# Places for raw weights apart, and six down matmuls between a slab's last two products

## The chip, the cores and the metric

The kernel runs on one core of a Trainium2 chip. It is timed in microseconds of device time, as the median of several runs. A profiled execution has its own time, and its trace gives the start and end of each instruction: TensorE (PE) multiplies, VectorE (DVE) and ScalarE (ACT) do elementwise work, GpSimd (POOL) does little here, and SyncE (SP) issues the loads from memory. Each engine takes its instructions strictly in one order.

## The reference

Two layers, each of an FFN, a mixer and a second FFN, every one followed by a residual sum and a layer norm. The sequence has 512 rows, the model width is 1024, the FFN width 2816.

```python
for l in range(DEPTH):                       # DEPTH = 2
    h = 0.5 * _swiglu(x, w_gate[l, 0], w_up[l, 0], w_down[l, 0])
    x = _layernorm(ALPHA * x + h, ...)
    h = _mixer(x, w_in[l], ..., w_out[l])    # convolution, LRU and windowed attention side by side
    x = _layernorm(ALPHA * x + h, ...)
    h = 0.5 * _swiglu(x, w_gate[l, 1], w_up[l, 1], w_down[l, 1])
    x = _layernorm(ALPHA * x + h, ...)

def _swiglu(x, wg, wu, wd):
    return (silu(x @ wg) * (x @ wu)) @ wd
```

All is float32. Gate and up are 1024 x 2816, down is 2816 x 1024, w_in 1024 x 1792 (14 column tiles of 128), w_out 1024 x 1024.

## The kernel before

**Split weights.** A float32 product is made of three products of a faster type. Each weight tile comes from memory as a raw tile of 128 x 1024 floats (512 KB). `split` makes its high part on ScalarE (`wh`, a cast, L131) and its low part on VectorE (`wl`, raw minus high, L132). Activations are held as high and low parts too (xT, sT, hH and hL). A product is then low weight by high activation, high weight by low activation, and high by high.

**Places.** `wpool` has 15 places of 128 x 1024 floats, which raw tiles, high and low parts, sums of raw tiles and partial results (`o`) share. `tpool` has 7 such places, for the raws of the gate and up weights and for scratch. PSUM has 8 banks of 128 x 512.

**Gate and up.** The FFN columns are handled as 11 pairs of blocks, in three slabs of 4, 4 and 3 pairs. One pair n takes seven products, named p1, p2, q6, p5, p7, p4, q3 (`run`), each of 24 matmuls of 128 x 256 (L482 to L484) on sums of weight blocks and of activation blocks. Their weights are prepared some steps ahead (`prep`): a sum of raws on VectorE (L420) where there is one, and a split. p1, q6, p7 and p4 of a pair add up in the same bank: between them ScalarE copies what stands there (L511, L516, L518, L521). p4 and q3 of a pair come after p1 of the next pair, except at a slab's end, where p7, p4 and q3 of the last pair follow each other directly. `finish` then makes silu(gate) times up and splits it into hH and hL.

**Down.** After a slab's products, each of its blocks f of 128 rows of w_down is loaded and split (`load_rows`), and `rowmm` multiplies it with the four row blocks t of the activations, six matmuls of 128 x 512 for each (L106): two with hL and the high weight, then four with hH, by the low and the high weight in turn. The sums of a slab stand in eight banks, two for each t, and all of them were taken at once, behind q3. In an FFN's last slab the last four blocks of w_down (RESIDENT) are held in place, and `tail` calls `rows(t)` for one t after another, takes the norm of that row block (L290 to L306) and transposes it (L138) for the next stage, whose first weights are loaded in between (`nxt.load`).

**Order.** The program is written in one order, and a scheduler sets from it, before the kernel runs, the order on each engine. So an instruction can stand at another place than the text has it, and loads are issued on SyncE's queue as their places come free.

Of the kernel before, what the change touches and what calls it, by code (L numbers as in the profile page):

```python
# [11 lines left out]
F32 = mybir.dt.float32  # L12
# [6 lines left out]
P = 128  # L19
D = 1024  # L20
S = 512
NT = S // P
# [29 lines left out]
def tile_hymba(  # L52
# [26 lines left out]
    nc = tc.nc  # L79

    cpool = ctx.enter_context(tc.tile_pool(name="cpool", bufs=1))
    wpool = ctx.enter_context(tc.tile_pool(name="wpool", bufs=15))
    hpool = ctx.enter_context(tc.tile_pool(name="hpool", bufs=1))
    xpool = ctx.enter_context(tc.tile_pool(name="xpool", bufs=1))
    tpool = ctx.enter_context(tc.tile_pool(name="tpool", bufs=7))
# [6 lines left out]
    def nm(s):  # L92
        uid[0] += 1
        return f"{s}_{uid[0]}"

    def bank():
        return psum.tile([P, 512], F32, tag="ps", name=nm("ps"))
# [7 lines left out]
    def mm(o, a, b, start, stop):  # L105
        nc.tensor.matmul(o, a, b, start=start, stop=stop)  # L106
# [27 lines left out]
    def transposed(dst, q, j, src):  # L134

        pt = bank()
        for c in range(4):
            nc.tensor.transpose(pt[:, c * P:(c + 1) * P], src[:, c * P:(c + 1) * P], ident)  # L138
        sl = slice(j * P, j * P + P)
        split(dst[q][:, 0, :, sl], dst[q][:, 1, :, sl], pt.rearrange("p (c t) -> p c t", c=4))  # L140
# [179 lines left out]
    class Start:  # L320
# [6 lines left out]
        def load(self, n=1, pool=None):  # L327
            for _ in range(n):
                self.pairs.append(self.thunks.pop(0)(pool))
# [32 lines left out]
                    mm(pb[:, lo:hi], wh[:, k, :], mh, False, k == KC - 1)  # L362

    def fetch_raw(src):
        raw = wpool.tile([P, D], F32, tag="w", name=nm("raw"))
        nc.sync.dma_start(raw if len(src.shape) == 2 else raw.rearrange("p (k f) -> p k f", k=KC), src)
        return raw

    def load(src, pool=None, raw=None):
        raw = fetch_raw(src) if raw is None else raw  # L370
        if pool is None:
            hi = wpool.tile([P, D], F32R, tag="w", name=nm("wh"))
            lo = wpool.tile([P, D], F32R, tag="w", name=nm("wl"))
        else:
            hi = tpool.tile([P, D], F32R, tag="t", name=nm("wh"))
            lo = tpool.tile([P, D], F32R, tag="t", name=nm("wl"))
        split(hi, lo, raw)
        return hi, lo
# [5 lines left out]
        pair = load(cols(src, c), pool, raw)  # L384
        return [w.rearrange("p (k f) -> p k f", k=KC) for w in pair]

    def load_rows(src, c, pool=None):
        return load(src[c * P:(c + 1) * P, :], pool)

# [62 lines left out]
    def rowmm(ys, a, w, first, last):  # L454
        ah, al = a
        wh, wl = w
        for hf in range(2):
            sl = slice(hf * 512, (hf + 1) * 512)
            mm(ys[hf], al, wh[:, sl], first, False)
        for hf in range(2):  # L460
            sl = slice(hf * 512, (hf + 1) * 512)
            mm(ys[hf], ah, wl[:, sl], False, False)
            mm(ys[hf], ah, wh[:, sl], False, last)

    def ffn(l, i, idx, start, nxt, last, hooks={}):
        wd = w_down[l, i]
# [8 lines left out]
        def product(step, n, pb, first):  # L475
            src, q = A[step]
            wh, wl = pairs[n].ready.pop(step)
            for g in range(2):
                o = pb[:, g * HALF:(g + 1) * HALF]
                for k in range(4):  # L480
                    st = first and g == 0 and k == 0
                    nc.tensor.matmul(o, wl[:, g, k, :], src[q][:, 0, k, :], start=st, stop=False, skip_group_check=True)  # L482
                    nc.tensor.matmul(o, wh[:, g, k, :], src[q][:, 1, k, :], start=False, stop=False, skip_group_check=True)  # L483
                    nc.tensor.matmul(o, wh[:, g, k, :], src[q][:, 0, k, :], start=False, stop=k == 3, skip_group_check=True)  # L484

        for si, (n0, n1) in enumerate(SLABS):
            fin = si == len(SLABS) - 1
            f0, f1 = 2 * n0, 2 * n1
            hH = hpool.tile([P, HMAX, S], F32R, tag="hA", name=nm("hH"))
            hL = hpool.tile([P, HMAX, S], F32R, tag="hB", name=nm("hL"))  # L490

            def finish(n, which, tile_, s0):

                v = tile_.rearrange("p (b g s) -> p b g s", b=2, g=2)
                nc.scalar.activation(v[:, :, 0, :], v[:, :, 0, :], AF.Silu)
                nc.vector.tensor_tensor(v[:, :, 0, :], v[:, :, 0, :], v[:, :, 1, :], op=ALU.mult)  # L496
                f = 2 * (n - n0)
                sl = (slice(None), slice(f, f + 2), slice(s0, s0 + HALF))
                split(hH[sl], hL[sl], v[:, :, 0, :])

            def run(step, n):
                if step in ("p1", "p2", "p5"):
                    acc[step, n] = bank()
                pb = acc[{"p1": "p1", "q6": "p1", "p7": "p1", "p4": "p1", "p2": "p2", "p5": "p5", "q3": "p5"}[step], n]
                product(step, n, pb, step in ("p1", "p2", "p5"))
                if step == "p1":
                    outs[n] = [wpool.tile([P, D], F32, tag="w", name=nm("o")) for _ in range(2)]
                oa, ob = outs[n]
                lo, hi = slice(0, 512), slice(512, 1024)
                if step == "p1":  # L510
                    nc.scalar.copy(oa[:, lo], pb)  # L511
                elif step == "p2":
                    nc.vector.tensor_tensor(oa[:, lo], pb, oa[:, lo], op=ALU.add)
                    acc.pop(("p2", n))
                elif step == "q6":
                    nc.scalar.copy(oa[:, hi], pb)  # L516
                elif step == "p7":
                    nc.scalar.copy(ob[:, hi], pb)  # L518
                    nc.vector.tensor_tensor(ob[:, hi], acc["p5", n], ob[:, hi], op=ALU.subtract)
                elif step == "p4":  # L520
                    nc.scalar.copy(ob[:, lo], pb)  # L521
                    finish(n, 1, ob, HALF)
                elif step == "q3":
                    nc.vector.tensor_tensor(oa[:, hi], pb, oa[:, hi], op=ALU.subtract)
                    finish(n, 0, oa, 0)
                    acc.pop(("p5", n))
                    acc.pop(("p1", n))
                    outs.pop(n)

            m4 = []  # L530
            first = n0 + 1 if si == 0 else n0
            if si == 0:
# [18 lines left out]
            seq = []  # L551
# [5 lines left out]
            for m, (step, n) in enumerate(seq):  # L557
                while ready < min(len(seq), m + 1 + AHEAD):
                    st, k = seq[ready]
                    pairs[k].prep(st)  # L560
                    ready += 1
                    if st == "p5" and k + 1 < n1:
                        pairs[k + 1].raw(0, 0)
                        pairs[k + 1].raw(1, 0)
                run(step, n)
                if m4:
                    transposed(sT, 2, 2 - len(m4), m4.pop(0))
                if step == "q3" and n in hooks:
                    hooks[n]()
            if fin:  # L570
                extra.pop()
            ys = [[bank(), bank()] for _ in range(NT)]

            def hpair(f, t):
                return hH[:, f - f0, t * P:(t + 1) * P], hL[:, f - f0, t * P:(t + 1) * P]

            flow = f1 - RESIDENT if fin else f1
            for f in range(f0, flow):
                w = load_rows(wd, f)
                for t in range(NT):  # L580
                    rowmm(ys[t], hpair(f, t), w, f == f0, f == f1 - 1)
            if not fin:
                for t in range(NT):
                    for hf, sl in enumerate(HS):
# [2 lines left out]
                continue  # L587
            coef = ln_coef(idx)
            ws = [load_rows(wd, f) for f in range(flow, f1)]
            if nxt:  # L590
                nxt.load(3)
                nxt.load(1, None)

            def rows(t):
                for w, f in zip(ws, range(flow, f1)):
                    rowmm(ys[t], hpair(f, t), w, f == f0, f == f1 - 1)
                return ys[t]
# [3 lines left out]
    def mixer(l, idx, start, nxt):  # L601
# [305 lines left out]
        for u in range(U + 2):  # L907
            if u < U:
                scores(u)
            if u < 2:  # L910
                query(2 + u)
            if SLAB_FROM <= u < SLAB_FROM + 4:
                wo.append(load_rows(w_out[l], 4 + u - SLAB_FROM))
            if 0 <= u - 2 < U:
                weighted(u - 2)
            if u - 3 in closes:
                attn_out(closes[u - 3], wo)
            if 0 <= u - 1 < U:
                transpose_p(u - 1)
            point()  # L920
            if u < U:
                normalise(u)
# [7 lines left out]
    for l in range(DEPTH):  # L930
        phases += [(ffn, (l, 0, 3 * l), ffn_start(l, 0)), (mixer, (l, 3 * l + 1), mixer_start(l)),
                   (ffn, (l, 1, 3 * l + 2), ffn_start(l, 1))]
# [61 lines left out]
```

## Time and profile before

| | before |
|---|---|
| median of 3 runs | 1774.04 us (1771.74 to 1775.43) |
| profiled execution | 1780.14 us, span 1778.4 us |
| TensorE clock granted in it | 0.987 of full |
| TensorE busy | 1720.0 us, 97% |
| VectorE busy | 1278.1 us, 72% |
| ScalarE busy | 821.1 us, 46% |
| loaded from memory | 171.33 MB |

The span is from the first to the last instruction of the trace. A row of a timeline gives the start in the span and the duration, then the engine, the line, the operation and its tiles; in brackets stands how long the engine had been idle and what ended that. Lines of the profile are those of the kernel before. SPq is SyncE's queue as it issues loads.

### The profile page before, as it was taken

To read this page: it belongs to the slowest core of one execution; us is meant where nothing else is said; L and a number is where in the kernel's file an instruction comes from. 1 tells how busy PE (TensorE), PEld (TensorE's weight loads), DVE (VectorE), ACT (ScalarE), POOL (GpSimd) and SP (SyncE) were. 2 spreads that over 40 slices of the span, in tenths; PEclk is the share of its full clock that TensorE was granted. 3 is DMA by queue.
4 is the path that set the end of the run, shared out by engine and by line. 5 is a ranking of instruction groups with operands and counts; after the bars stand their busy time and mean duration, and the time that the engine had idled before them with its cause. 6 is when DMAs were issued, how large, how long until landed. Compare 5 with 4: busy or idle time off the path is not lost. (4 is left out here: it accounts for less than half of the span.)

```text
span 1778.4 us, 27912 instructions
## 1 busy us (share of the span) xinstructions
PE 1720.0 (97%) x11538; PEld 1546.7 (87%) x11538; DVE 1278.1 (72%) x1777; ACT 821.1 (46%) x1224; POOL 44.0 (2%) x76
## 2 busy tenths in 40 slices
PE   8999999999999999999999999999999999999997
PEld 8988989887679989979889899898875799898896
DVE  5856856779877856747688567576898877577485
ACT  4543533543854543434445335254457445255252
POOL 0200000010000000000000000000000000000000
PEclk9999999999899999999999999999998999999999
DMA  5341542321222432422324324223311244235122
GB/s 157 109 142 57 167 135 72 119 81 45 98 84 75 127 131 72 129 85 72 107 84 131 131 71 128 87 72 110 111 59 58 73 124 144 65 104 163 45 94 72
DMA packets 236840, 177.34 MB, mean 100 GB/s; under 512 B 9524, under 2 KB 219561, under 8 KB 236713
## 3 DMA queue, kind: packets, MB, share of 16 engines
q1 hardware_dynamic: 236712, 175.55, 32.1%
q8 instruction: 91, 1.49, 0.3%
q14 instruction: 37, 0.30, 0.0%
HBM read 171.33 MB, written 3.67 MB: 98 GB/s over the span
## 5 line engine op out<-in xcount | busy, mean ns | idle before, releaser
L132 DVE TENSOR_TENSOR wl<-raw,wh 128x1024 fp32r<-128x1024 f32 x268 | 324.9, 1221 | 156.3 <-ACT wh L131 114.2
L482 PE MATMUL ps<-xT,wl 128*128 128x256 f32 x1280 | 355.5, 278 | 10.8 <-ACT o L518 9.8
L483 PE MATMUL ps<-xT,wh 128*128 128x256 f32 x1280 | 353.3, 276 | 0.0
L484 PE MATMUL ps<-xT,wh 128*128 128x256 f32 x1280 | 353.2, 276 | 0.0
L131 ACT CAST wh<-raw 128x1024 fp32r<-128x1024 f32 x268 | 278.5, 1048 | 132.7 <-DMA raw<-in_ffn_w_down_dram 69.8
L132 DVE TENSOR_TENSOR wl<-t,wh 128x1024 fp32r<-128x1024 f32 x160 | 195.8, 1226 | 143.4 <-ACT wh L131 117.7
L106 PE MATMUL ps<-wl,hH 128*128 128x512 f32 x704 | 276.5, 393 | 4.2 <-DVE wl L132 4.2
L106 PE MATMUL ps<-wh,hH 128*128 128x512 f32 x704 | 275.5, 391 | 0.0
L482 PE MATMUL ps<-sT,wl 128*128 128x256 f32 x960 | 264.8, 276 | 4.9 <-ACT o L511 4.9
L484 PE MATMUL ps<-sT,wh 128*128 128x256 f32 x960 | 264.1, 275 | 0.0
L483 PE MATMUL ps<-sT,wh 128*128 128x256 f32 x960 | 264.1, 275 | 0.0
L131 ACT CAST wh<-t 128x1024 fp32r<-128x1024 f32 x160 | 167.6, 1055 | 201.2 <-DVE t L420 166.0
L482 PEld LDWEIGHTS ps<-xT,wl 128*128 128x128 f32 x1280 | 241.2, 188 | 15.2 <-ACT o L518 12.1
L483 PEld LDWEIGHTS ps<-xT,wh 128*128 128x128 f32 x1280 | 241.3, 188 | 0.3
L484 PEld LDWEIGHTS ps<-xT,wh 128*128 128x128 f32 x1280 | 241.1, 188 | 0.0
L106 PE MATMUL ps<-wh,hL 128*128 128x512 f32 x704 | 218.6, 392 | 4.7 <-ACT wh L131 4.7
L106 PE MATMUL ps<-xT,wh 128*128 128x256 f32 (+1 forms) x960 | 214.3, 318 | 2.2 <-DVE xT L132 2.2
L482 PEld LDWEIGHTS ps<-sT,wl 128*128 128x128 f32 x960 | 180.3, 188 | 6.6 <-ACT o L511 5.8
L484 PEld LDWEIGHTS ps<-sT,wh 128*128 128x128 f32 x960 | 180.2, 188 | 0.0
L483 PEld LDWEIGHTS ps<-sT,wh 128*128 128x128 f32 x960 | 180.2, 188 | 0.0
L106 PEld LDWEIGHTS ps<-xT,wh 128*128 128x128 f32 x960 | 159.2, 191 | 17.1 <-DVE xT L132 3.2
L106 PEld LDWEIGHTS ps<-wl,hH 128*128 128x128 f32 x704 | 132.9, 189 | 35.2 <-DVE wl L132 7.7
(165 smaller groups left out, 2345.7 us busy)
## 6 DMA issues: line engine op xcount, KB each, us to landing
raw<-in_ffn_w_down_dram SPq DMA_DIRECT2D x88, 512.0 KB
raw<-in_ffn_w_gate_dram SPq DMA_DIRECT2D x160, 256.0 KB
raw<-in_ffn_w_up_dram SPq DMA_DIRECT2D x160, 256.0 KB
raw<-in_w_in_dram SPq DMA_DIRECT2D x28, 512.0 KB
raw<-in_w_out_dram SPq DMA_DIRECT2D x16, 512.0 KB
raw<-in_ffn_w_gate_dram SPq DMA_DIRECT2D x8, 512.0 KB
raw<-in_ffn_w_up_dram SPq DMA_DIRECT2D x8, 512.0 KB
t<-in_ln_g_dram SPq DMA_DIRECT2D x6, 512.0 KB
```

The source lines that it names most:

```text
L106: nc.tensor.matmul(o, a, b, start=start, stop=stop)
L131: nc.scalar.copy(hi, src)
L132: nc.vector.tensor_tensor(lo, src, hi.bitcast(F32), op=ALU.subtract)
L482: nc.tensor.matmul(o, wl[:, g, k, :], src[q][:, 0, k, :], start=st, stop=False, skip_group_check=True)
L483: nc.tensor.matmul(o, wh[:, g, k, :], src[q][:, 1, k, :], start=False, stop=False, skip_group_check=True)
L484: nc.tensor.matmul(o, wh[:, g, k, :], src[q][:, 0, k, :], start=False, stop=k == 3, skip_group_check=True)
```

## The change

Four things. Raw tiles of w_down, w_in, w_out and of an FFN's first gate and up columns get two places of their own (`rpool`); `wpool` has 16 places, for all else. The first two raws of a slab's w_down are sent for at p1 of the slab's last pair. The split of block f0 is written ahead of p7 and the one of f0+1 behind q3. The six matmuls of (f0, t = 0) stand between p7 and p4, and the banks of a t are taken when it is first needed; behind q3 come the other t of f0 and f0+1 in a written order, then the blocks from f0+2 on as before.

```diff
-    wpool = ctx.enter_context(tc.tile_pool(name="wpool", bufs=15))
+    wpool = ctx.enter_context(tc.tile_pool(name="wpool", bufs=16))
+    rpool = ctx.enter_context(tc.tile_pool(name="rpool", bufs=2))
...
     def fetch_raw(src):
-        raw = wpool.tile([P, D], F32, tag="w", name=nm("raw"))
+        raw = rpool.tile([P, D], F32, tag="r", name=nm("raw"))
...
-    def load_rows(src, c, pool=None):
-        return load(src[c * P:(c + 1) * P, :], pool)
+    def load_rows(src, c, pool=None, raw=None):
+        return load(src[c * P:(c + 1) * P, :], pool, raw)
...
+            ys = {}
+            early = {}
+
+            def hpair(f, t):
+                return hH[:, f - f0, t * P:(t + 1) * P], hL[:, f - f0, t * P:(t + 1) * P]
+
+            def down(f, t):
+                if t not in ys:
+                    ys[t] = [bank(), bank()]
+                rowmm(ys[t], hpair(f, t), early[f], f == f0, f == f1 - 1)
...
+                if (step, n) == ("p1", n1 - 1):
+                    first_raw = {f: fetch_raw(wd[f * P:(f + 1) * P, :]) for f in (f0, f0 + 1)}
+                if m == len(seq) - 3:
+                    early[f0] = load_rows(wd, f0, None, first_raw.pop(f0))
+                if m == len(seq) - 2:
+                    down(f0, 0)
                 run(step, n)
...
-            ys = [[bank(), bank()] for _ in range(NT)]
-
-            def hpair(f, t):
-                return hH[:, f - f0, t * P:(t + 1) * P], hL[:, f - f0, t * P:(t + 1) * P]
-
             flow = f1 - RESIDENT if fin else f1
-            for f in range(f0, flow):
-                w = load_rows(wd, f)
+            early[f0 + 1] = load_rows(wd, f0 + 1, None, first_raw.pop(f0 + 1))
+            for f, t in ((f0, 1), (f0, 2), (f0 + 1, 0), (f0 + 1, 1), (f0 + 1, 2), (f0, 3), (f0 + 1, 3)):
+                down(f, t)
+            for f in range(f0 + 2, flow):
+                early[f] = load_rows(wd, f)
                 for t in range(NT):
-                    rowmm(ys[t], hpair(f, t), w, f == f0, f == f1 - 1)
+                    down(f, t)
```

What the scheduler makes of it is seen in the order of instructions on an engine: line, operation, what is written and what is read, with the shape. (Below line 80 the changed kernel's lines are one higher than before, so L131 and L132 are L132 and L133 there.)

The first slab's end on ScalarE, before. `wh_1042` is p4's weight, `wh_1071` q3's, `wh_1204` the first of w_down; L518 copies p7's result and L521 p4's.

```order
L131 CAST wh_1042<-t_121_1040 128x1024
L131 CAST wh_1071<-raw_920 128x1024
L518 COPY o_913<-ps_887 128x512
L521 COPY o_913<-ps_887 128x512
L131 CAST wh_1204<-raw_1202 128x1024
```

The same place with the change. `wh_1049` is p4's weight, `wh_1078` q3's, `wh_1107` block f0 of w_down, `wh_1213` f0+1, `wh_1267` f0+2; L519 and L522 are the copies.

```order
L132 CAST wh_1049<-t_123_1047 128x1024
L132 CAST wh_1078<-raw_927 128x1024
L132 CAST wh_1107<-raw_890 128x1024
L519 COPY o_920<-ps_894 128x512
L132 CAST wh_1213<-raw_892 128x1024
L132 CAST wh_1267<-raw_1265 128x1024
L522 COPY o_920<-ps_894 128x512
```

f0's cast has moved ahead of p7's copy and stands third, behind the casts for p4 and q3; those of f0+1 and f0+2 have moved ahead of p4's copy. VectorE's subtractions stand in the same order.

On TensorE at that place, before, p7's last matmul is followed directly by p4's first:

```order
L483 MATMUL ps_887<-sT_142,wh_1010 128x256
L484 MATMUL ps_887<-sT_142,wh_1010 128x256
L482 MATMUL ps_887<-xT,wl_1043 128x256
L483 MATMUL ps_887<-xT,wh_1042 128x256
L484 MATMUL ps_887<-xT,wh_1042 128x256
```

With the change (`ps_1137` and `ps_1138` are the banks of t = 0, `ps_1217` and `ps_1218` those of t = 1):

```order
L485 MATMUL ps_894<-sT_145,wh_1017 128x256
L107 MATMUL ps_1137<-wh_1107,hL_159 128x512
L107 MATMUL ps_1138<-wh_1107,hL_159 128x512
L107 MATMUL ps_1217<-wh_1107,hL_159 128x512
L107 MATMUL ps_1218<-wh_1107,hL_159 128x512
L107 MATMUL ps_1137<-wl_1108,hH_158 128x512
L107 MATMUL ps_1137<-wh_1107,hH_158 128x512
L107 MATMUL ps_1138<-wl_1108,hH_158 128x512
L107 MATMUL ps_1138<-wh_1107,hH_158 128x512
L483 MATMUL ps_894<-xT,wl_1050 128x256
```

Two matmuls of (f0, t = 1) have been put in as well: eight of 512 columns stand between p7 and p4.

The tail of the first FFN on VectorE, with the change. The L291 rows are the first row block's residual sums, L294 to L307 its norm, the L133 rows splits of the next stage's first weights:

```order
L133 TENSOR_TENSOR wl_3567<-raw_3564,wh_3566 128x1024
L291 SCALAR_TENSOR_TENSOR t_3606,zs_3607<-ps_3412,xs 128x512
L133 TENSOR_TENSOR wl_3573<-raw_3570,wh_3572 128x1024
L291 SCALAR_TENSOR_TENSOR t_3606,zs_3607<-ps_3413,xs 128x512
L133 TENSOR_TENSOR wl_3579<-raw_3576,wh_3578 128x1024
L294 TENSOR_SCALAR nmean_3610<-zs_3607 128x1
L305 SCALAR_TENSOR_TENSOR xs<-t_3606,nmean_3610,t_3530 128x512 x2
```

Before, the sums of two row blocks came together, with one split behind them; now the first block's sums stand alone, with splits between them.

The kernel's end on VectorE, before, has the sums of row blocks 0 and 1 together:

```order
L290 SCALAR_TENSOR_TENSOR t_16986,zs_16987<-ps_16866,xs 128x512
L290 SCALAR_TENSOR_TENSOR t_16986,zs_16987<-ps_16867,xs 128x512
L290 SCALAR_TENSOR_TENSOR t_17026,zs_17027<-ps_16868,xs 128x512
L293 TENSOR_SCALAR nmean_16990<-zs_16987 128x1
L290 SCALAR_TENSOR_TENSOR t_17026,zs_17027<-ps_16869,xs 128x512
L304 SCALAR_TENSOR_TENSOR xs<-t_16986,nmean_16990,t_16934 128x512 x2
```

With the change each row block's norm is through before the next one's sums:

```order
L291 SCALAR_TENSOR_TENSOR t_16989,zs_16990<-ps_16819,xs 128x512
L291 SCALAR_TENSOR_TENSOR t_16989,zs_16990<-ps_16820,xs 128x512
L294 TENSOR_SCALAR nmean_16993<-zs_16990 128x1
L305 SCALAR_TENSOR_TENSOR xs<-t_16989,nmean_16993,t_16937 128x512 x2
L307 SCALAR_TENSOR_TENSOR xs<-xs,rs_16995,t_16938 128x512 x2
L291 SCALAR_TENSOR_TENSOR t_17029,zs_17030<-ps_16889,xs 128x512
```

On TensorE the four resident blocks of w_down are taken for one row block after the other there, where those of row blocks 0 and 1 stood mixed.

## The prediction

> **What bounds the kernel now.** I read the page first, then the waits of TensorE, then the timelines of TensorE, ScalarE and VectorE around one slab end, then those around the last norms. The page:
>
> ```profile
> PE 1720.0 (97%) x11538; PEld 1546.7 (87%) x11538; DVE 1278.1 (72%) x1777; ACT 821.1 (46%) x1224; POOL 44.0 (2%) x76
> ```
>
> TensorE is busy nearly always, and the change removes no matmul. So it can only win from TensorE's stops, and from what lies behind its last matmul. The waits of TensorE (total, times, longest) list the stops:
>
> ```profile
> PE ps L482 <- ACT o L518: 9.8, 12, 1.7
> PE ps L138 <- DVE xs L306: 6.7, 5, 1.6
> PE ps L138 <- DMA xs<-in_x_dram: 6.0, 2, 4.5
> ...
> PE ps L106 <- ACT wh L131: 4.7, 7, 2.1
> PE ps L106 <- DVE wl L132: 4.2, 8, 0.5
> ...
> PE ps L106 <- DVE xT L132: 2.2, 4, 0.9
> ...
> PE ps L482 <- DVE wl L132: 1.0, 4, 0.3
> ```
>
> Rows 1, 4, 5 and 7 are the slab ends: twelve waits for p7's copy, then those of the first down matmuls for their weights. They make 19.7 us, plus about 0.17 at each stop, because a gap counts from the end of a 0.28 us matmul whose successor normally starts 0.11 us after its start. Start to start, the twelve slab ends lose 26.5 us by my count. The first of them, on TensorE, ScalarE, VectorE and SyncE's queue:
>
> ```profile
> 94.80 0.28 PE L483 MATMUL ps<-sT,wh 128*128 128x256 f32 x1
> 94.91 0.28 PE L484 MATMUL ps<-sT,wh 128*128 128x256 f32 x1
> 95.92 0.39 PE L482 MATMUL ps<-xT,wl 128*128 128x256 f32 x1 [0.73 <-ACT o L518]
> ...
> 98.78 0.28 PE L482 MATMUL ps<-sT,wl 128*128 128x256 f32 x1
> ...
> 101.39 0.28 PE L484 MATMUL ps<-sT,wh 128*128 128x256 f32 x1
> 102.54 0.73 PE L106 MATMUL ps<-wh,hL 128*128 128x512 f32 x2 [0.88 <-ACT wh L131]
> 103.80 0.50 PE L106 MATMUL ps<-wl,hH 128*128 128x512 f32 x1 [0.53 <-DVE wl L132]
> 104.14 0.39 PE L106 MATMUL ps<-wh,hH 128*128 128x512 f32 x1
> 104.37 0.39 PE L106 MATMUL ps<-wl,hH 128*128 128x512 f32 x1
> ```
>
> ```profile
> 92.90 1.06 ACT L131 CAST wh<-t 128x1024 fp32r<-128x1024 f32 x1 [2.43 <-DVE t L420]
> 93.86 1.05 ACT L131 CAST wh<-raw 128x1024 fp32r<-128x1024 f32 x1
> 95.28 0.59 ACT L518 COPY o<-ps 128x512 f32<-128x512 f32 x1 [0.38 <-PE ps L484]
> ...
> 101.44 1.04 ACT L131 CAST wh<-raw 128x1024 fp32r<-128x1024 f32 x1 [1.88 <-DMA raw<-in_ffn_w_down_dram]
> ```
>
> ```profile
> 93.99 1.23 DVE L132 TENSOR_TENSOR wl<-t,wh 128x1024 fp32r<-128x1024 f32 x1 [1.18 <-ACT wh L131]
> 95.13 1.22 DVE L132 TENSOR_TENSOR wl<-raw,wh 128x1024 fp32r<-128x1024 f32 x1
> 96.27 0.68 DVE L519 TENSOR_TENSOR o<-ps,o 128x512 f32<-128x512 f32 x1
> ```
>
> ```profile
> 96.83 1.42 SPq L366 DMA_DIRECT2D raw<-in_ffn_w_down_dram  x1
> ...
> 114.56 0.33 SPq L366 DMA_DIRECT2D raw<-in_ffn_w_down_dram  x1
> ```
>
> p7 is issued out at 95.02 (94.91 plus a step of 0.11). p4 adds into the same bank, so it waits for the copy: 0.90 lost. q3 ends at 101.50, but the first w_down raw was sent for only at 96.83, its cast starts 4.61 later, and TensorE loses 1.04 for the cast and 0.80 for the subtraction. Together 2.7 to 2.9 us.
>
> **The change part by part.** *Six down matmuls ahead of p4.* The copy is now covered: it runs while TensorE works on f0. But these matmuls need f0's own split, and the orders put that split last of three on both engines: behind p4's and q3's. In the rows above ScalarE is through q3's cast at 94.91, so f0's cast ends about 95.95: TensorE waits 0.93 from p7's end. It then does the four hL products (0.227 each, the step from 104.14 to 104.37): until 96.87. VectorE is through q3's subtraction at 96.35 (start 95.13, 1.22), so f0's ends about 97.52: 0.65 more. Four products, since the scheduler has put eight down matmuls there and not six: p4 starts at 98.43. From p7's end that is 3.41, of which 8 x 0.227 = 1.82 is work: lost 1.6. The wait has changed its name from the copy to f0's split. Behind q3 nothing is waited for any more, since f0 and f0+1 are split by then. So 2.87 becomes 1.61 here.
>
> The same reckoning elsewhere hangs on when q3's preparation ends against p7. Two other slab ends, the first of them the last slab of an FFN:
>
> ```profile
> 330.61 1.04 ACT L131 CAST wh<-raw 128x1024 fp32r<-128x1024 f32 x1
> 331.89 1.22 DVE L132 TENSOR_TENSOR wl<-raw,wh 128x1024 fp32r<-128x1024 f32 x1
> ...
> 748.09 1.22 DVE L132 TENSOR_TENSOR wl<-raw,wh 128x1024 fp32r<-128x1024 f32 x1
> ```
>
> With p7 ending at 330.31 and 747.57 the losses go from 1.91 to 3.09 and from 5.33 to 2.02. The eight slab ends that are not an FFN's last lose 21.8 before and 13.6 after. The four last ones have no wait behind q3 today (their raws came early), so only the copy, 0.92 in three of them: 4.7 before, 7.7 after. Sum: 26.5 to 21.3, **gain 5.2**. If the split came first on both engines, all of it would go; if it came a whole subtraction later, 12 x 1.14 more would be lost: bounds +26 and -9.
>
> *Two raw places.* A raw place is free again only after the subtraction, so loads go in pairs. One load takes 114.56 to
>
> ```profile
> 118.14 1.05 ACT L131 CAST wh<-raw 128x1024 fp32r<-128x1024 f32 x1 [3.63 <-DMA raw<-in_ffn_w_down_dram]
> ```
>
> that is 3.58 until its cast, up to 4.61 above, then 1.05 and 1.22: 5.9 to 6.9 for two, 2.9 to 3.4 each. A down step takes 24 x 0.227 = 5.45, so the stream keeps up: f0+2 is sent for at 97.5, ready near 104.5, and needed only at about 113. Cost 0 while that cover of 9 us lasts. The first raws of the next slab now stand in SyncE's queue ahead of that slab's later pair raws, and wait for the splits of the last w_down blocks, here at 121.1 and 122.3 with
>
> ```profile
> 119.84 2.48 DVE L132 TENSOR_TENSOR wl<-raw,wh 128x1024 fp32r<-128x1024 f32 x2 [4.07 <-PE ps L106]
> ...
> 128.73 0.38 SPq L412 DMA_DIRECT2D raw<-in_ffn_w_gate_dram  x1
> ```
>
> before the pair raw behind them was sent: 0, with 6 us of cover.
>
> *The inner tails (three).* rows(0) is now finished alone, 5.45 us ahead of rows(1), where both ended together. But two to four splits of the next stage's first loads stand before the first norm is through on VectorE, and they come by pairs. Before:
>
> ```profile
> 359.77 0.69 DVE L290 SCALAR_TENSOR_TENSOR t<-ps,xs 128x512 f32<-128x512 f32 x1 [11.50 <-PE ps L106]
> ```
>
> My reckoning with 3.58 per load gives 2.6 us of wait at the first transposes and 0.4 to 0.6 at the second, 3.2 a tail, where rows 2 and 6 of the waits and their restarts make 9.6 for three today. So 0. With loads of 4.6 it would be 2 more per tail; if the loads were in time, up to 3.2 less.
>
> *The kernel's end.* Before, rows(0) and rows(1) end together, and four norms run one after another on VectorE:
>
> ```profile
> 1766.26 0.39 PE L106 MATMUL ps<-wh,hH 128*128 128x512 f32 x1
> ```
>
> ```profile
> 1755.81 0.69 DVE L290 SCALAR_TENSOR_TENSOR t<-ps,xs 128x512 f32<-128x512 f32 x1 [12.37 <-PE ps L106]
> ...
> 1770.57 0.68 DVE L290 SCALAR_TENSOR_TENSOR t<-ps,xs 128x512 f32<-128x512 f32 x1
> ...
> 1773.81 1.41 DVE L306 SCALAR_TENSOR_TENSOR xs<-xs,rs,t 128x512 f32<-128x512 f32 x2 [0.84 <-POOL rs L297]
> ```
>
> The last matmul ends at 1766.65, the last norm at 1775.22, the span at 1778.4: 11.75 behind TensorE. From 1755.81 to 1775.22 is 4.85 a norm, and a row block of four weights takes 4 x 6 x 0.227 = 5.45: with the blocks finished one by one, three norms hide under matmuls. Left are one norm (1770.57 to 1775.22, 4.65, and 0.61 for its other half's sum) and the store, 3.2: 8.5. **Gain 3.3**; at least 0, at most 4.
>
> *Start and mixers.* Two of the first weights now go ahead of x's third block: 0 to one transfer, 1.4 (the 96.83 row): I take 0.5 lost. In the mixers
>
> ```profile
> raw<-in_w_in_dram SPq DMA_DIRECT2D x28, 512.0 KB
> raw<-in_w_out_dram SPq DMA_DIRECT2D x16, 512.0 KB
> ```
>
> go by pairs as well, where up to 15 places were open. A projection of one column tile takes 5.45, above 3.4, so 0, with one late load (4.6) per mixer as the bound on the one side and 2 per mixer gained on the other.
>
> **Sum:** -5.2 - 3.3 + 0.5 = -8.0: the profiled execution's 1780.1 becomes 1772. It lies 6.1 above the median of the runs, so the median 1774.0 becomes **1766**.
>
> **Rivals.** *A, the stops are cured.* If f0's split were in time, all 26.5 and the 3.3 would go: 1774 - 30 = 1744. For it speaks that 16 + 2 places replace 15; against it that q3's subtraction ends 1.2 us behind p7 in the rows above, with f0's behind that. It decides if ScalarE and VectorE run over 2 us earlier against TensorE than now. The Trainium skill (Perfetto Trace Analysis, Optimization Strategy) says that the same gap repeating on the engine that should be full can mean too few SBUF or PSUM places. By that, the added places would give this result; the trace disagrees at p4, where the releaser is a copy, and agrees only behind q3, where a raw came late.
>
> *B, two places are too few: slower.* Where a load's cast comes 4.6 and not 3.6 after its issue, each of three inner tails loses 2 more (6), and each mixer waits once for a load that was there before (9.2): -8 + 15.2 = +7, 1781. It decides from about 4.3. For it: the 4.61 measured with other transfers beside it, and engines that go strictly in order, so that one late raw stops every copy and norm behind it. Against it: 3.58 where the queue is idle, as in tails and mixers.
>
> *C, waits only change names.* The slab ends win 2 or less because the last slabs lose more than 3, and the end wins 1 or 2 because the norms now meet splits: 1771 to 1777. For it: the four last slabs already lose by my own count.
>
> **How the numbers follow.** About 0.2%, 3.5 us, is what can be told from no change. The forecast (1760 to 1770.5) has 0.50, A 0.10, C 0.18, B 0.22. So faster 0.60, same 0.18, slower 0.22. The range reaches from a third of the way to A to the near part of B, 1755 to 1780, which leaves out most of A and some of B.
>
> **What would show it.** In the waits: no row of p4 for L518's copy; in its place twelve waits of the hL products for ACT's wh (0.3 to 1.9 each) and twelve of the hH products for DVE's wl (about 0.7); none behind q3; about 21 us in all. At the end: the last VectorE norm about 5.3 behind the last matmul, where it is 8.6. In the tails: waits for xs of 2 to 3 us in total per tail. I am wrong if these waits are missing or twice as long, or if new waits for w_in or w_out show up in the mixers.

## The result

The changed kernel takes 1762.33 us (median of 4 runs, 1761.57 to 1765.92), the kernel before 1774.48 (median of 4, 1771.74 to 1775.43). The ratio is 0.9934, with a 95% interval from 0.9922 to 0.9947: 12.2 us faster, where 8.0 were forecast. The profiled execution of the changed kernel took 1762.13 us, with a span of 1760.4; that is its median, while the one of before lay 5.7 above its own. So the two traces differ by 18.0 us and the medians by 12.2.

The page of the changed kernel, where its engines are as busy as before:

```profile
PE 1709.4 (97%) x11538; PEld 1541.6 (88%) x11538; DVE 1279.2 (73%) x1777; ACT 819.8 (47%) x1224; POOL 39.5 (2%) x76
```

The waits of its TensorE, total, times and longest (its lines are one higher than before up to L525, and 12 to 18 higher behind that):

```profile
PE ps L107 <- ACT wh L132: 11.2, 12, 2.1
PE ps L139 <- DVE xs L307: 6.7, 3, 2.7
PE ps L139 <- DMA xs<-in_x_dram: 6.0, 2, 4.6
PE ps L107 <- DVE wl L133: 5.2, 12, 0.5
...
PE ps L107 <- ACT xT L132: 2.3, 1, 2.3
...
PE ps L483 <- DVE wl L133: 1.0, 4, 0.3
```

No product waits for p7's copy any more. In its place stand, at each of the twelve slab ends, one wait of the hL products for ScalarE's `wh` and one of the hH products for VectorE's `wl`. The first slab end, on TensorE, ScalarE and VectorE (start, duration, idle time before and what ended it):

```profile
95.84 0.28 PE L485 MATMUL ps<-sT,wh 128*128 128x256 f32 x1
96.88 1.20 PE L107 MATMUL ps<-wh,hL 128*128 128x512 f32 x4 [0.76 <-ACT wh L132]
98.52 0.50 PE L107 MATMUL ps<-wl,hH 128*128 128x512 f32 x1 [0.45 <-DVE wl L133]
...
99.56 0.28 PE L483 MATMUL ps<-xT,wl 128*128 128x256 f32 x1
```

```profile
94.84 1.98 ACT L132 CAST wh<-raw 128x1024 fp32r<-128x1024 f32 x2
96.73 0.58 ACT L519 COPY o<-ps 128x512 f32<-128x512 f32 x1
```

```profile
94.97 1.23 DVE L133 TENSOR_TENSOR wl<-t,wh 128x1024 fp32r<-128x1024 f32 x1 [1.12 <-ACT wh L132]
96.11 2.35 DVE L133 TENSOR_TENSOR wl<-raw,wh 128x1024 fp32r<-128x1024 f32 x2
```

The two casts from 94.84 are q3's and f0's, the two subtractions from 96.11 likewise. p7 is issued out at 95.95. p4 starts at 99.56, 3.61 later, of which 1.82 is work; 1.79 is lost.

The end of the kernel on TensorE and VectorE:

```profile
1751.97 0.39 PE L107 MATMUL ps<-wh,hH 128*128 128x512 f32 x1
```

```profile
1751.95 0.69 DVE L291 SCALAR_TENSOR_TENSOR t<-ps,xs 128x512 f32<-128x512 f32 x1 [0.17 <-PE ps L107]
...
1755.80 1.42 DVE L307 SCALAR_TENSOR_TENSOR xs<-xs,rs,t 128x512 f32<-128x512 f32 x2 [0.85 <-POOL rs L298]
```

One norm is left behind the last matmul.

**Where the time went.** The program has the same 11,538 matmuls before and after. So the time from the n-th to the m-th matmul can be compared directly. The second trace of before is that of run e0 below.

| Part of the program (matmul counts) | before | before, 2nd trace | changed | changed minus first |
|---|---|---|---|---|
| start and first products (0 to 620) | 80.10 | 80.04 | 80.92 | +0.8 |
| products with the bias table (930 to 1480) | 72.18 | 70.69 | 73.88 | +1.7 |
| eight slab ends that are not an FFN's last | | | | -8.8 |
| four last slabs with their tails | | | | +2.0 |
| first mixer's second half (2900 to 3340) | 100.03 | 97.53 | 95.35 | -4.7 |
| second mixer's (8560 to 9050) | 115.48 | 113.93 | 110.01 | -5.5 |
| behind the last matmul's start | 12.10 | 12.09 | 8.38 | -3.7 |

These sum to -18.2; the spans differ by -18.0. The mixers, costed at nothing, won 10.2 against the first trace of before and 6.1 against the second. At the slab ends the sum came out near the forecast, but not by stops alone. 4.8 of the 8.8 were won at one end, near 756 in the span, where TensorE waits 2.1 for f0's cast in the kernel before. Behind that wait the first trace shows a granted clock of 0.50 for 6.8 us (the window's busy times, then clock, DMA share and GB/s), in which the step between two down matmuls is 0.43 us and not 0.227:

```profile
757.00:763.80 6.80, 6.27 (x16) 4.88 (x16) 6.46 (x9) 5.53 (x7) 0.00 (x0) 0.50 0.64 233
```

The two other traces with the order of before show 3.4 us at 0.50 there, the changed kernel none. In the changed kernel the clock stood at 0.50 for 3.4 us from 335.3, behind a wait of 2.1 at the first FFN's last slab.

### The profile page after: what moved, and what is told of

Read it like the earlier page. It is cut to its first block, busy times and chain, and to the rows that moved or that the text cites. A ratio compares the mean times of both kernels' runs of the same rounds, so it can differ in the third digit from the quotient of the medians.

```text
span 1760.4 us, 27877 instructions
## 1 busy us (share of the span) xinstructions
PE 1709.4 (97%) x11538; PEld 1541.6 (88%) x11538; DVE 1279.2 (73%) x1777; ACT 819.8 (47%) x1224; POOL 39.5 (2%) x76
## 4 chain that ended last, share of the span: by engine, by line
PE 53%; DVE 27%; ACT 10%; DMA 6%; issue 3%; SPq 0%; POOL 0%; DVEq 0%; ACTq 0%; POOLq 0%
PE ps L107 40%; DVE wl L133 11%; DVE t L421 8%; ACT wh L132 6%; PE ps L483 4%; PE ps L484 4%; PE ps L485 4%; DMA raw<-in_ffn_w_up_dram 4%; DVE hL L133 2%; PE ps L139 2%; DVE o L497 2%; DMA raw<-in_ffn_w_down_dram 1%; ACT t L858 1%; DVE o L525 1%; DMA raw<-in_w_in_dram 1%
## 5 line engine op out<-in xcount | busy, mean ns | idle before, releaser
L133 DVE TENSOR_TENSOR wl<-raw,wh 128x1024 fp32r<-128x1024 f32 x268 | 324.4, 1221 | 153.0 <-ACT wh L132 152.0
L132 ACT CAST wh<-raw 128x1024 fp32r<-128x1024 f32 x268 | 277.4, 1048 | 190.0 <-DMA raw<-in_ffn_w_down_dram 123.8
L133 DVE TENSOR_TENSOR wl<-t,wh 128x1024 fp32r<-128x1024 f32 x160 | 195.9, 1226 | 143.6 <-ACT wh L132 143.5
L107 PE MATMUL ps<-wl,hH 128*128 128x512 f32 x704 | 276.5, 393 | 5.2 <-DVE wl L133 5.2
L132 ACT CAST wh<-t 128x1024 fp32r<-128x1024 f32 x160 | 168.4, 1055 | 233.5 <-DVE t L421 186.2
L107 PE MATMUL ps<-wh,hH 128*128 128x512 f32 x704 | 275.1, 391 | 0.0
L107 PE MATMUL ps<-wh,hL 128*128 128x512 f32 x704 | 217.1, 392 | 11.2 <-ACT wh L132 11.2
L107 PE MATMUL ps<-xT,wh 128*128 128x256 f32 (+1 forms) x960 | 212.8, 317 | 0.0
L107 PEld LDWEIGHTS ps<-xT,wh 128*128 128x128 f32 x960 | 158.2, 190 | 14.0 <-issue 0.5
L107 PEld LDWEIGHTS ps<-wh,hL 128*128 128x128 f32 x704 | 131.3, 188 | 40.3 <-ACT wh L132 13.5
```

Of the source, the lines that this page charges most:

```text
L132: nc.scalar.copy(hi, src)
L133: nc.vector.tensor_tensor(lo, src, hi.bitcast(F32), op=ALU.subtract)
```

## The experiments

Two theories stood against each other at first. Mine: the six matmuls only rename the wait, because f0's split comes last of three; the places won what was won behind q3 and in the mixers. The rival: the six matmuls win, and the places serve them. Each ratio is against the kernel before, timed beside that run. The medians of the kernel before lie between 1773.7 and 1777.2 from one experiment to the next, so a difference in us between two kernels that were not timed together is good to some 4 us.

**e0, the kernel before once more**, with no edit, for a second trace.

> The kernel before, unchanged, for a second profiled execution of it. In its first one the two attention stretches run at a granted clock of 0.55 and 0.77 for 10 and 22 us, and the mixers take 10.2 us longer than with the change, though the medians differ by 12.2 and the spans by 18.0. If the clock falls there because of the order of its attention, the same two stretches show it again and the mixers lose 9 to 11 us against the changed kernel. If it was that one execution, they show 0.9 to 1.0 here, and the span comes out 4 to 6 us shorter, near 1773.

One run: 1776.58 us, span 1774.8. The stretch of the first mixer was at full clock this time. First and second trace, a window of 10 us each (busy times of TensorE, weight loads, VectorE, ScalarE, GpSimd, then the granted clock, the DMA share and GB/s):

```profile
475.00:485.00 10.00, 9.74 (x25) 5.37 (x25) 7.94 (x27) 7.32 (x24) 0.00 (x0) 0.55 0.14 52
```

```profile
475.00:485.00 10.00, 8.09 (x32) 4.80 (x33) 9.42 (x34) 8.64 (x25) 0.00 (x0) 1.00 0.15 52
```

Without the low clock the mixer took 97.5 instead of 100.0, still 2.2 over the changed kernel's. The second mixer took 113.9, 3.9 over, but there the clock had fallen again, to 0.50 for 6.8 us. So neither expectation held whole: part of the 10.2 was the clock, and at most 6.1 were not.

**e1, the places alone.**

```diff
-    wpool = ctx.enter_context(tc.tile_pool(name="wpool", bufs=15))
+    wpool = ctx.enter_context(tc.tile_pool(name="wpool", bufs=16))
+    rpool = ctx.enter_context(tc.tile_pool(name="rpool", bufs=2))
...
-        raw = wpool.tile([P, D], F32, tag="w", name=nm("raw"))
+        raw = rpool.tile([P, D], F32, tag="r", name=nm("raw"))
```

> The two raw places and the sixteenth shared one alone; nothing stands between p7 and p4. My theory (the cover only renames the wait, and what was won behind q3 and in the mixers comes from the places): p4 waits for the copy again, 12 x 0.9 = 11 us, nothing is waited for behind q3, mixers, tails and end are those of the changed kernel; so the slab ends lose 11 where the changed kernel loses 21, and the time is about 1753, 9 below the changed kernel. Rival (the six matmuls are what wins, the places only serve them): 1768 to 1775, close to the kernel before.

1751.31 us, ratio 0.9856 (0.9832 to 0.9880). The waits:

```profile
PE ps L483 <- ACT o L519: 9.8, 12, 1.6
PE ps L139 <- DVE xs L307: 8.3, 3, 3.2
```

The twelve waits for the copy are back, and nothing waits for a down weight. The places alone win 26 us, twice what the whole change wins, and about what I expected (1753). With them there, the six matmuls as the change places them cost some 11. (e1 has the sixteenth shared place too; it was not tried apart from the other two.)

**e2, the move alone**: the changed kernel with its raws in the 15 shared places of before.

```diff
-    wpool = ctx.enter_context(tc.tile_pool(name="wpool", bufs=16))
-    rpool = ctx.enter_context(tc.tile_pool(name="rpool", bufs=2))
+    wpool = ctx.enter_context(tc.tile_pool(name="wpool", bufs=15))
...
-        raw = rpool.tile([P, D], F32, tag="r", name=nm("raw"))
+        raw = wpool.tile([P, D], F32, tag="w", name=nm("raw"))
```

> The early raws, the early splits and the six matmuls alone, with the raws in the 15 shared places as before. My theory: slab ends as in the changed kernel (21 us), mixers as before, so about 1766 to 1770. Rival (the six matmuls are what wins): 1762 to 1764, as the changed kernel. If the raws held longer in the shared places delay the pairs' weights, above 1775.

1750.59 us, ratio 0.9853 (0.9830 to 0.9876). Both theories missed: the move alone wins as much as the places alone, and each alone twice what they win together. The trace says where. Its waits, then its first slab end:

```profile
PE ps L106 <- ACT wh L131: 8.6, 12, 1.6
...
PE ps L106 <- DVE wl L132: 1.5, 4, 0.5
...
PE ps L138 <- DVE xs L306: 1.4, 3, 0.5
```

```profile
95.19 0.96 PE L106 MATMUL ps<-wh,hL 128*128 128x512 f32 x3 [0.61 <-ACT wh L131]
96.00 0.28 PE L482 MATMUL ps<-xT,wl 128*128 128x256 f32 x1
...
96.59 0.28 PE L484 MATMUL ps<-xT,wh 128*128 128x256 f32 x1
96.83 0.50 PE L106 MATMUL ps<-wl,hH 128*128 128x512 f32 x1
```

With other places the scheduler sets another order: three hL products, six matmuls of p4, then the hH products, whose low weights are ready by then. The second wait is gone at the eight slab ends that are not an FFN's last. And the inner tails wait 1.4 in all, where the changed kernel waits 6.7: their raws are not a chain of two. The mixers are those of before (97.0 and 113.9). A second trace of this kernel was to show whether that is the order or one execution:

> The early raws, splits and the six matmuls with the raws in 15 shared places once more, for a second profiled execution of the old attention order without any place apart. If the order alone decides, its first mixer takes 97 to 101 and its second 113 to 116 between the same matmuls, where the kernels with raws apart took 95.1 to 97.8 and 110.0 to 111.0.

It took 97.1 and 113.9 there, as in the first trace of e2. The 97.1 lies within both ranges that I had named, so it does not tell them apart; the 113.9 does, but with the clock at 0.50 for 6.8 us again.

**e4, f0's split first.** The changed kernel with the split of f0 written three steps earlier.

```diff
-                if m == len(seq) - 3:
+                if m == len(seq) - 6:
                     early[f0] = load_rows(wd, f0, None, first_raw.pop(f0))
```

> The changed kernel with f0's split written three steps earlier, so that it stands ahead of p4's and q3's on ScalarE and VectorE; six matmuls, not eight, then stand between p7 and p4. My theory (the slab end loses what f0's split is late): f0 is split by p7's end, p4's subtraction ends about 1.2 us after it, under 1.36 us of matmuls; the slab ends lose 0 to 4 us instead of 21, time 1742 to 1747. Rival (VectorE is full in the product steps, and one split more there delays the next product): the wait moves to p4's or q3's low weights, 0.9 to 1.2 at each slab end, 1756 to 1762.

1747.10 us, ratio 0.9833 (0.9806 to 0.9860), about 15 below the changed kernel; a little over my 1742 to 1747. The scheduler now leaves six matmuls between p7 and p4. The waits of the slab ends, then the tails':

```profile
PE ps L483 <- ACT o L519: 2.4, 4, 0.9
...
PE ps L139 <- DVE xs L307: 9.6, 3, 3.4
```

No down matmul waits for a weight. Four waits for the copy are left. The tails wait 2.9 longer than in the changed kernel.

**e3, f0's split second**, between p4's and q3's, to tell the place of the split from the number of matmuls.

```diff
-                if m == len(seq) - 3:
+                if m == len(seq) - 5:
```

> The changed kernel with f0's split one place earlier, between p4's and q3's on ScalarE and VectorE, and six matmuls between p7 and p4. My theory: f0's cast is ready at p7's end and its subtraction about 1.2 us after it, while the two hL products take 0.45: 0.8 lost at each slab end, about 10 in all, against 21 (f0 third) and near 5 (f0 first); time 1750 to 1753. Rival (what e4 won came from six matmuls in place of eight): slab ends as with f0 first, 1746 to 1748.

1752.02 us, ratio 0.9878 (0.9855 to 0.9900). Six matmuls as in e4, and twelve waits for the low weight:

```profile
PE ps L107 <- DVE wl L133: 8.5, 12, 0.7
...
PE ps L107 <- ACT wh L132: 2.0, 4, 1.1
```

That is 0.7 each, near the 0.8 expected; the four waits for the cast were not expected. So f0 third, second and first on VectorE leaves 16.4, 10.5 and 2.4 us of waits at the slab ends, the last of them for the copy. The second and the first place have the same six matmuls, so it is the place that counts: the slab end loses what f0's split is late.

**e5, three more shared places and nothing else.**

```diff
-    wpool = ctx.enter_context(tc.tile_pool(name="wpool", bufs=15))
+    wpool = ctx.enter_context(tc.tile_pool(name="wpool", bufs=18))
```

> The kernel before with 18 shared places instead of 15, as many as the changed kernel has in all, and nothing else. TensorE's order is then that of before, matmul for matmul. My theory (what the places win comes from raws that have a place apart: they are sent for early, and the attention's order changes): the first w_down raw still stands in SyncE's queue behind the pair raws, whose places are others, so slab ends, mixers and tails stay, 1770 to 1777. Rival (three places more is what counts): slab ends lose 11 to 14 instead of 26.5, 1758 to 1764.

1777.02 us, ratio 1.0019 (1.0008 to 1.0030). As many places as the changed kernel has, all shared, win nothing:

```profile
PE ps L482 <- ACT o L518: 9.0, 12, 1.6
...
PE ps L106 <- ACT wh L131: 5.6, 7, 1.5
...
PE ps L106 <- DVE wl L132: 4.2, 8, 0.5
```

So it is not the number of places that e1 wins by. What it has besides is that raws stand apart.

**e6, f0's split first with the raws in 18 shared places**: e4 without `rpool`, `wpool` at 18.

> f0's split first as in e4, but with the raws in the shared places, 18 of them. My theory: the slab ends lose 5 as in e4, each inner tail 0.5 to 1 instead of 3.3 (no chain of two raws ahead of the first norm), and the mixers are those of before, 2 to 4 longer each: 1742 to 1746. Rival (the two places apart cost nothing in the tails, the norm order does): tails as in e4, 1750 to 1755.

1741.74 us, ratio 0.9819 (0.9800 to 0.9839). The slab ends and the inner tails wait little, as expected:

```profile
PE ps L138 <- DVE xs L306: 1.3, 3, 0.5
...
PE ps L482 <- ACT o L518: 0.3, 1, 0.3
```

The mixers went back to 101.1 and 113.1. In the first of them the clock fell again, to 0.67 over ten microseconds, so its 5.9 over e4 are more than the 2 to 4 expected; the second stayed at 1.00:

```profile
465.00:475.00 10.00, 8.21 (x22) 4.17 (x22) 8.74 (x30) 7.48 (x24) 0.00 (x0) 0.67 0.07 15
```

**e9, e4 with the next stage's first raws in shared places**, the others apart. The same is done for the first gate and up tiles of an FFN (`ffn_start`).

```diff
+    def wraw(src):
+        raw = wpool.tile([P, D], F32, tag="w", name=nm("raw"))
...
-        return Start([lambda pool, c=c: load_cols(w_in[l], c, pool) for c in (2, 0, 3, 1)])
+        return Start([lambda pool, c=c: load_cols(w_in[l], c, pool, wraw(cols(w_in[l], c))) for c in (2, 0, 3, 1)])
```

> e4 with the raws of each next stage's first weights (four tiles) in shared places, all other raws in the two places apart. My theory: the attention keeps its new order, so mixers as in e4; the inner tails no longer wait for a chain of raws: 0.5 to 1.5 each instead of 3.3, and the start gets its x blocks first as before, 0.5 to 1 less. So 6 to 9 below e4: 1738 to 1742. Rival (VectorE is short of time in the tails, whatever the raws): 1745 to 1748, as e4.

1746.93 us, ratio 0.9844 (0.9821 to 0.9867): a miss, no better than e4. The inner tails fell only to between 1.5 and 2.1 each, and the mixers grew, to 97.8 and 111.0. Each has a wait of 1.7 for an attention tile `t`, where e4 waits 0.7 at most, and one of 1.1 at the transposes that follow, which e4 does not have:

```profile
PE ps L139 <- DVE xs L307: 7.7, 6, 2.1
PE ps L107 <- ACT t L892: 7.7, 10, 1.7
```

The resident w_down raws still come in pairs ahead of the tail. (Lines of e9 and e10 are six higher than before here: L524 is p7's copy, L522 q6's.) So the chain of two raws is only part of what the tails lose; how the rest divides was not tried.

**e10, e6 with two places apart for the mixers' raws alone.**

```diff
+    def apart(src):
+        raw = rpool.tile([P, D], F32, tag="r", name=nm("raw"))
...
-                    ahead[c] = load_cols(wl, c)
+                    ahead[c] = load_cols(wl, c, None, apart(cols(wl, c)))
```

The same is done for the four w_out blocks that are loaded in the attention; `wpool` has 16 places.

> e6 (f0's split first, raws in shared places) with two places apart for the raws of the mixers alone: those of w_in's column tiles after the first four, and of the four w_out blocks loaded in the attention; 16 shared places. TensorE's order is e6's everywhere but in the attention, where it is that of the changed kernel. My theory (the mixers' gain is the order that raws apart give there): slab ends and tails as in e6, mixers 2 to 6 shorter each, 1734 to 1739. Rival (the mixers' times differ by how the clock is granted in one execution, not by order): 1740 to 1744, as e6.

1737.29 us, ratio 0.9791 (0.9775 to 0.9807), 25 below the changed kernel: the lowest median of all, as expected, though its interval still overlaps e6's. TensorE's order differs from e6's in the attention alone, and the two mixer stretches take 96.8 and 110.2 in place of 101.1 and 113.1. The second is a fair comparison, with the clock at 1.00 in both: 2.8 won. In the first e6's clock had fallen, so those 4.3 are not the order's alone. Its largest waits at slab ends and at transposes (2.3 of the first row stand behind the two mixers, 1.3 in the three inner tails):

```profile
PE ps L139 <- DVE xs L307: 3.6, 5, 1.1
...
PE ps L488 <- ACT o L524: 1.1, 4, 0.3
PE ps L488 <- ACT o L522: 1.0, 1, 1.0
```

The mixers over all traces, by the order in which the attention stands on TensorE:

| | first mixer (2900 to 3340) | second (8560 to 9050) |
|---|---|---|
| raws shared: before twice, e5, e2 twice, e6 | 97.0 to 101.1 | 113.1 to 115.5 |
| of these, passes at a clock of 1.00 | 97.0 to 98.9 (e0, e5, e2 twice) | 113.1 (e5, e6) |
| raws apart: changed, e1, e3, e4, e9, e10 (all at 1.00) | 95.1 to 97.8 | 110.0 to 111.0 |

The six traces of each kind show one and the same order on TensorE in these stretches. At equal clock the second mixer is 2.0 to 3.1 us shorter with raws apart. In the first the ranges touch: the changed kernel, e1, e3 and e4 take 95.1 to 95.4, but e10 and e9 96.8 and 97.8, with waits of 1.4 and 1.7 for `t` late in the stretch where the others wait 0.3, and of 1.1 at the transposes.

## Why the prediction was right, and where it was not

**The slab ends: the mechanism was right, the gain in stops mis-sized.** The forecast was that the wait moves from the copy to f0's split, 0.93 for the cast and 0.65 for the subtraction at the first slab end. Measured, start to start, are 0.93 and 0.61. The waits sum to 11.2 and 5.2 us with 24 stops of 0.17 each, 20.5, where 21.3 was forecast. But the same count gives only 23.3 for the kernel before (18.7 and 27 stops), not 26.5: at one end (p7's end at 747.57) the forecast counted 5.33, where the stops make 3.9 and the rest is work at half clock. So in stops the change won 2.8 at the slab ends, where 5.2 was forecast: the eight ends went from 18.6 to 13.3, the four last slabs from 4.6 to 7.1 (forecast 4.7 to 7.7). From matmul to matmul the eight won 8.8 (forecast 8.2) and the four lost 4.7; most of the difference is the clock of those two traces, which had no term of its own in the sum. One row was misread: the four waits of L482 for VectorE's `wl`, 1.0 us, are not at slab ends. They stand at the start of an FFN's first whole pair, and the changed kernel has the same row. The slab-end waits of before were 18.7, not 19.7.

**Rival A: the stops are not cured by the change, but can be.** I gave as its condition that f0's split be in time, and e4 met it by moving one line. The Trainium skill (Perfetto Trace Analysis, Optimization Strategy) has such repeated gaps as a possible sign of too few places; here three more shared places gave a ratio of 1.0019 (e5), so the number of places was not the reason.

**Rival C had the right grain.** The last slabs lose, by 2.5 together. The end did not give back: 3.7 won, 3.3 forecast, with 4.9 from the last matmul's end to the last norm's end (forecast 5.3) and 3.1 more to the end of the span.

**The tails: near in sum, wrong in how.** Forecast was 3.2 us a tail, 9.6 together, as before. Measured are single waits of 1.5, 2.5 and 2.7 at the first transposes, 7.2 with their restarts, and none at the second ones. The chain that I costed is there. ScalarE waits for each of the four w_in raws in turn, and the splits on VectorE come about 3.1 apart (forecast 2.9 to 3.4):

```profile
350.32 1.05 ACT L132 CAST wh<-raw 128x1024 fp32r<-128x1024 f32 x1 [1.19 <-DMA raw<-in_w_in_dram]
353.57 1.05 ACT L132 CAST wh<-raw 128x1024 fp32r<-128x1024 f32 x1 [2.20 <-DMA raw<-in_w_in_dram]
356.30 1.05 ACT L132 CAST wh<-raw 128x1024 fp32r<-128x1024 f32 x1 [1.68 <-DMA raw<-in_w_in_dram]
359.69 1.05 ACT L132 CAST wh<-raw 128x1024 fp32r<-128x1024 f32 x1 [2.35 <-DMA raw<-in_w_in_dram]
```

```profile
359.12 0.69 DVE L291 SCALAR_TENSOR_TENSOR t<-ps,xs 128x512 f32<-128x512 f32 x1
...
360.77 1.23 DVE L133 TENSOR_TENSOR wl<-raw,wh 128x1024 fp32r<-128x1024 f32 x1 [0.96 <-ACT wh L132]
361.92 0.21 DVE L294 TENSOR_SCALAR nmean<-zs 128x1 f32<-128x1 f32 x1
```

The first norm stands behind the last of these splits, as forecast. What I costed at "0" is a price of its own all the same: e6 and e2, without that chain, have tails of 0.5.

**Rival B did not decide.** The loads of the tail came every 3.1 us, not later, so its condition was not met, and no mixer waited for a raw that had been there before.

**The step that failed is "A projection of one column tile takes 5.45, above 3.4, so 0".** It asked only whether raws arrive in time, and bounded the gain at 2 us per mixer. The places changed the order of the attention on TensorE. In one place of several a w_out product (`wh,yL`) of an earlier row block stands between two groups of attention products (`t,mix`). The changed kernel:

```profile
476.89 1.12 PE L107 MATMUL ps<-t,mix 128*128 128x512 f32 x2
477.46 0.79 PE L107 MATMUL ps<-wh,yL 128*128 128x512 f32 x1
478.09 1.02 PE L107 MATMUL ps<-t,mix 128*128 128x512 f32 x2
```

The same place in e2, which has the order of before, at a clock of 1.00:

```profile
473.29 1.98 PE L106 MATMUL ps<-t,mix 128*128 128x512 f32 x4 [0.94 <-ACT t L886]
474.71 1.02 PE L106 MATMUL ps<-wh,yL 128*128 128x512 f32 x2
```

Four products `mix,t` also stand earlier among the projections, and the transposes `ident,t` are dealt out otherwise. At these places e2 waits 0.7, 1.3, 0.8, 1.0 and 0.9 in the first mixer, the changed kernel 0.2, 0.3 and 0.6; later it waits 1.7 more, which e2 does not. At a clock of 1.00 the order is worth 1.7 to 3.5 us against the changed kernel's first mixer (97.0 to 98.9 against 95.3) and 3.1 in the second (113.1 against 110.0); e10 against e6 shows 2.8 for the second with the rest of the order the same. Where the clock fell, the old order takes 1 to 4 more. The new order was there to be seen before any run: I compared the orders at slab ends and tails, and not in the attention. So the total fell into the range partly by luck: 5 to 7 of the 12.2 came from a term that was put at 0, and without it the change would have won less than the 8.0 forecast.

**The start** lost 0.8 (forecast 0.5): the wait for the transposed x in the row `PE ps L107 <- ACT xT L132: 2.3` is new, in place of one of 0.9. In the products with the bias table the changed kernel shows 1.7 us more. That is no effect of the change: the same kernel e2 took 72.2 there in one execution and 73.8 in another, and the granted clock over the ten microseconds from 172 lies between 0.51 and 0.83 in the twelve traces, though TensorE is busy for 9.97 at least.

**What stays open.** The forecast -8.0 less 5 to 7 in the mixers would be -13 to -15, the second trace of before gives -14.4, and the medians -12.2. The runs of the kernel before spread from 1771 to 1783; its clock in the attention was seen in two of these executions only.

## What to carry to other kernels

Work put ahead of a waiting instruction covers the wait only if its own inputs are ready by then: before inserting it, look up where its preparation stands on each preparing engine, and move that first. In a scheduled program a change of pools can re-order engines far from the edit; compare the whole order, stage by stage, and cost every place where it differs. Two gains that each hold alone need not add up, so measure each half of a combined change by itself.

## What the runs showed of the hardware that was not expected

The granted clock fell in the attention though no single wait was long. In the first trace of before TensorE was busy 7.91 of the ten microseconds up to 475, with no wait above 1.3 us, and then ran at 0.55 for the next ten:

```profile
465.00:475.00 10.00, 7.91 (x35) 3.84 (x32) 9.81 (x36) 9.69 (x31) 0.00 (x0) 0.93 0.17 54
```

With the old order of the attention the clock fell so in six of twelve passes (two mixers in six traces: before twice, e2 twice, e5, e6), not always at the same mixer. The first mixer of before took 2.5 us more in the trace where it fell. In the new order it stayed at 1.00 in all twelve passes of its six traces. The busy share over ten microseconds alone does not decide it. In e2's first mixer, with the old order, TensorE was busy for less than above, and the clock stayed at 1.00:

```profile
460.00:470.00 10.00, 6.94 (x29) 3.36 (x28) 9.78 (x33) 9.76 (x31) 0.00 (x0) 1.00 0.18 52
```

So it did in e9, with the new order, at 7.53 in the ten from 490. What decides stays open.

In all twelve traces the clock also fell once between 168 and 175, with TensorE busy throughout. There stand 14 matmuls with only 33 rows of weights one after another, and the fall comes 2.8 to 5.7 us after the first of them. The changed kernel's:

```profile
168.69 6.59 PE L107 MATMUL ps<-t,t 33*128 33x384 f32 x14
```

That the few rows are the reason is not shown.

The Trainium skill (TensorE: Matmul & The Clock Gate, Part 1) has the clock halved after an idle window of about 3.4 us, and tells of frequent short idles between groups of matmuls as another way; here no wait in the attention was half as long as that window, so the falls fit the second better.
